# Taking the experts of a mixture-of-experts layer in an order computed on the chip

## The chip, the cores and the metric

The kernel runs on one core of one Trainium2 chip. The metric is device microseconds of one execution, from launch to end. One further execution was taken by the hardware profiler; its times count from the first instruction, and "span" is the time from the first to the last instruction. In the profile PE is the matrix engine (PEld its weight loads), DVE, ACT and POOL are the vector, scalar and general engines, and SP is the engine whose queue issues nearly all DMA loads here.

## The reference

One layer: a token mixer (gated delta rule and state-space heads), then a mixture of 32 experts, then a final RMSNorm. The mixer is not touched by the change. What matters is the expert layer, over 256 tokens of width 1024:

```
logits = (hf @ router_w + router_b).astype(jnp.float32)
top_logit, top_idx = lax.top_k(logits, TOP_K)          # TOP_K = 4 of N_EXPERTS = 32
gates = jax.nn.softmax(top_logit, axis=-1)
...
def expert_block(args):
    xb, e = args
    y = clamped_swiglu(xb @ w_gu[e] + b_gu[e])         # 1024 -> 2 x 1024, float32
    return y @ w_down[e] + b_down[e]                   # 1024 -> 1024
...
y_rows = y_rows * row_gate[:, None].astype(y_rows.dtype)
out = jax.ops.segment_sum(y_rows, row_tok, num_segments=n_tok + 1)[:n_tok]
```

256 tokens with 4 experts each make 1024 assignments, 32 to an expert on average; how many an expert gets is known only when the router has run. The sum over experts does not depend on the order in which they are taken.

## The kernel before

**Weights.** Each expert has 12 MiB of float32 weights, read once: eight loads of 1 MiB for gate and up (`w<-in_moe_w_gu_dram` in the profile), then four of 1 MiB for down (`w<-in_moe_w_down_dram`). `seq` lists all 384 loads, expert 0 to expert 31. `fetch(n)` issues them in that order on SP's queue (line L87 in the profile), each into the next of 20 slots of 1 MiB in turn (`SLOTS`). A load has to wait until the weights that stood in its slot have been used by PE. With 12 loads to an expert, 20 slots hold one whole expert and the first eight loads of the next. The last load is issued in two halves. The source address of each load is a constant of the program.

**The main loop.** It takes the experts one after the other, `e` from 0 to 31. `Block.pick` and `gather` select up to `CAP` = 64 tokens of an expert by a one-hot matrix made from `pos` (the token's place within the expert, 0 if it isn't there); `features` turns them into `xe`; `gate_up` runs k = 0 to 7 over the eight loads of gate and up (tiles `pG`, `pU`), and with the last use of each its slot is free; `swiglu` and `hidden` make `hTe`; `down` goes over the other four loads (tile `pY`), `result` and `scatter` add the result to the sum `acc`. The work on the next expert's tokens and the last one's result stands between `gate_up` and `down`, so that PE has something to do while `swiglu` runs. After the last expert there is the final norm and the store.

**Extra blocks.** An expert with more than 64 tokens needs a second pass. `xblk` holds, for each expert, the number of extra blocks of `XCAP` = 32 tokens, computed at the router from the counts; engines load it into registers, four experts at a time (`extra_blocks`). At the start of iteration `e` a conditional branch (L1465) runs `extra(e)` if that number is positive: gather, gate and up, swiglu, down, result and scatter of up to 32 more tokens, one step after the other, with the same weights of expert `e`. It stands ahead of the main `gate_up` of `e`, so all 12 slots of the expert stay taken until the main pass has used them. In the profile its down product goes to tile `pw` instead of `pY`. (`rest`, at the end, is for experts with more than 96 tokens.)

**Names.** `id3[:, e]` picks the expert's row of the biases, `gt[:, t, e]` holds the weights of the tokens for the expert.

Of the kernel before, what the change touches and what calls it, by code (L numbers as in the profile page):

```python
# [22 lines left out]
FT = mybir.dt.float32  # L23
I32 = mybir.dt.int32
BF = mybir.dt.bfloat16
FR = mybir.dt.float32r
AF = mybir.ActivationFunctionType
OP = mybir.AluOpType
PSUM = bass.MemoryType.PSUM
AX = mybir.AxisListType  # L30
# [6 lines left out]
NE = 32  # L37
EPS = 1e-6
CAP = 64
XCAP = 32  # L40
XMAX = (SEQ - CAP) // XCAP
RING = 8

SLOTS = ("w5", "w6", "w7", "w0", "w1", "g", "odd", "c", "hT", "s2", "s1", "even", "xd", "s3", "w2", "w3", "w4", "yh",
         "yl", "xT")
# [3 lines left out]
def trunk_kernel(ctx: ExitStack, tc: tile.TileContext, x, c, ada_w, ada_b, norm1_g, norm2_g, w_in,  # L49
# [3 lines left out]
    nc = tc.nc  # L53
    V, S, T, G = nc.vector, nc.scalar, nc.tensor, nc.gpsimd
# [18 lines left out]
    last_load = [None]  # L73
# [16 lines left out]
    gu_src = moe_w_gu.rearrange("o e (k p) n -> p (o e) k n", p=128)  # L90
    dn_src = moe_w_down.rearrange("o e (p k) n -> p (o e) k n", p=128)
    seq = [(e, i) for e in range(n_static) for i in range(12)]
    W = {}

    def fetch(n):

        while len(W) < min(n, len(seq)):
            e, i = seq[len(W)]
            src = gu_src[:, e, i] if i < 8 else dn_src[:, e, 2 * i - 16:2 * i - 14]
            W[e, i] = load(src, [2 * D] if i < 8 else [2, D], SLOTS[len(W) % len(SLOTS)], True,  # L100
                           2 if len(W) == len(seq) - 1 else 1)

# [9 lines left out]
    def ts(t):  # L112
        return slice(t * 128, t * 128 + 128)
# [47 lines left out]
    def tmp(n, dt=FT):  # L161
        taken[0] += n
        v = scratch[:, taken[0] - n:taken[0]]
        return v if dt is FT else v.bitcast(dt)
# [63 lines left out]
    V.tensor_tensor(x64, l64, s64, op=OP.bitwise_xor)  # L228
    l64f = const.tile([128, 64], FT)
    V.tensor_copy(l64f, l64)  # L230
    s64f = tmp(64)
    V.tensor_copy(s64f, s64)
    x64f = tmp(64)
# [41 lines left out]
    p = pg()  # L275
# [857 lines left out]
    dump("A2", A2)  # L1133


    id3 = const.tile([96, NE], BF)
    for j in range(3):
        V.tensor_copy(id3[32 * j:32 * j + 32], ident[0:NE, 0:NE])
# [82 lines left out]
    T.matmul(p[:, 0:32], before, sel[:, 0], start=True, stop=True)  # L1221
    T.matmul(p[:, 32:64], before, sel[:, 1], start=True, stop=False)
    posm = T.matmul(p[:, 32:64], ones, sel[:, 0], start=False, stop=True)


    nmax = fc.tile([1, 1], FT)
# [1 line left out]
    nblk = fc.tile([1, NE + 1], I32)  # L1228
    V.tensor_scalar(nblk[:, :NE], p[0:1, 64:96], float(CAP), float(XCAP - 1 - CAP), op0=OP.max, op1=OP.add)
    V.tensor_scalar(nblk[:, NE:], nmax, float(CAP), float(XCAP - 1 - CAP), op0=OP.max, op1=OP.add)  # L1230
    xblk = const.tile([1, NE + 2], I32)
    V.tensor_scalar(xblk[:, :NE + 1], nblk, XCAP.bit_length() - 1, None, op0=OP.arith_shift_right)
    V.tensor_scalar(xblk[:, NE + 1:], xblk[:, NE:NE + 1], 1.0, None, op0=OP.subtract)
    V.tensor_tensor(xblk[:, NE + 1:], xblk[:, NE + 1:], xblk[:, NE - 1:NE], op=OP.max)
    pos = rt("pos", pool=const)
    V.scalar_tensor_tensor(pos, p[:, :64].rearrange("p (t e) -> p t e", t=2), 1.0, sel, op0=OP.add, op1=OP.mult)
    V.tensor_tensor(gt, gt, sel, op=OP.mult)
# [16 lines left out]
    def pw(tag="pw"):  # L1254
        return pm.tile([128, 512], FT, name=tag, tag=tag)
# [135 lines left out]
    def extra_blocks(e):  # L1391


        n = min(e + GROUP, NE)
        return nc.values_load_multi_w_load_instructions(xblk[0:1, e:n + 2 * (n == NE)], min_val=0, max_val=XMAX)

    fetch(len(SLOTS))

# [2 lines left out]
            T.matmul(pacc[t][:, n], ident, xt[:, t, n * 512:n * 512 + 512], start=True, stop=True)  # L1401

    def block(e):
        return Block(lambda i: W[e, i], id3[:, e:e + 1])

    def extra_block(weights, pick, pcol, gcol):
        blk = Block(weights, pick, XCAP)
        blk.pick(pcol, gcol)
        blk.gather()
        blk.features()  # L1410
        blk.gate_up()
        blk.swiglu()
        blk.hidden()
        blk.down()
        blk.result()
        blk.scatter()

    def extra(e):
        pc = mk.tile([128, 2, 1], FT, name="pc")
        V.tensor_scalar(pc, pos[:, :, e:e + 1], float(CAP), None, op0=OP.subtract)  # L1420
        extra_block(lambda i: W[e, i], id3[:, e:e + 1], lambda t: pc[:, t], lambda t: gt[:, t, e:e + 1])

    def rest():

# [33 lines left out]
    for e in range(n_static):  # L1458
        fetch(12 * e + len(SLOTS))
        nxt = block(e + 1) if e + 1 < n_static else None  # L1460
        if nxt:
            nxt.pick(lambda t: pos[:, t, e + 1:e + 2], lambda t: gt[:, t, e + 1:e + 2])
        if e % GROUP == 0:
            nxs = extra_blocks(e)[1]
        with tc.If(nxs[e % GROUP if nxt else -1] > 0, label=f"more{e}", preferred_fallthrough_block=True):  # L1465
            if nxt:
                extra(e)
            else:
                with tc.If(nxs[e % GROUP] > 0):
                    extra(e)  # L1470
                with tc.If(nxs[-2] > 1):
                    rest()
        if not nxt:

            fgb = slot(SLOTS[4], "fgb")[:, :D]
            nc.sync.dma_start(fgb, final_g.rearrange("(o d) -> o d", o=1).to_broadcast([128, D]))
        if prev:
            prev.result()
        cur.gate_up()
        cur.swiglu()  # L1480

        if nxt:
            with tc.issue_after(cur.last.ins):
                tc.mark_branch_hint_location(f"more{e + 1}", engines=[nc.tensor.engine])
        if prev:
            with tc.issue_after(cur.last.ins):
                prev.scatter()
        if nxt:
            with tc.issue_after(cur.last.ins):
                nxt.gather()  # L1490
        cur.hidden()
        if nxt:
            nxt.features()
        cur.down()
        prev = cur
        cur = nxt
    if prev:
# [44 lines left out]
```

## Time and profile before

| | us |
|---|---|
| median of 3 runs | 1362.15 |
| the 3 runs | 1360.41, 1362.15, 1365.9 |
| the profiled execution | 1360.52 |
| its span | 1358.4 |
| start of the first expert's gate and up on PE, from the start of the span | 417.97 |
| end of the last matmul of the last expert's down | 1345.50 |
| PE busy | 1279.3 (94% of the span) |
| DVE, ACT busy | 541.0, 173.9 |
| moved by DMA | 470.21 MB, 346 GB/s over the span |

The first 418 us are the mixer and the router, the next 927 us are the 32 experts, and the last 13 us the final norm and the store. A busy PE in this profile can be a PE whose matmuls follow each other without a visible gap, whatever sets their pace, so the shares of busy time alone do not say what bounds the expert stage.

### The profile page before, as it was taken

The page shows a single profiled execution, that of the slowest core. Times are in us where ns is not written, and L with a number is a line of the kernel's source. Part 1 is how long each engine was busy: PE and PEld are TensorE (multiplying, and loading weights), DVE is VectorE, ACT ScalarE, POOL GpSimd, SP SyncE. Part 2 cuts the span into 40 slices and gives each one's busy share as a digit, 9 for nine tenths or more (in the row PEclk, how much of TensorE's full clock was granted, in tenths as well). Part 3 has the DMA queues.
Part 4 walks back from the last instruction along what each step waited for, and adds up shares of the span by engine and source line. Part 5 has one row for each costly group of instructions (what it writes and reads, how often), then busy time and mean ns, then how long its engine had stood idle before and what let it go on. Part 6 is the DMA issues. An engine that isn't in the chain of part 4 may idle for free. (4 is left out here: it accounts for less than half of the span.)

```text
span 1358.4 us, 18855 instructions
## 1 busy us (share of the span) xinstructions
PE 1279.3 (94%) x7520; PEld 625.9 (46%) x7521; DVE 541.0 (40%) x1555; ACT 173.9 (13%) x369; POOL 33.4 (2%) x46
## 2 busy tenths in 40 slices
PE   5999999999999999999998999998988999999996
PEld 3887787876553333333333333333333333333332
DVE  5797987444743223323322222222223223222322
ACT  1122222211210001000100001000000000000101
POOL 3010100000100000000000000000000000000000
PEclk9999999999998999999999999999999899999998
DMA  9986482316277999999999999999999999999991
GB/s 340 329 268 208 145 275 88 124 63 248 93 286 289 426 426 427 424 426 427 426 424 426 427 425 426 426 426 426 425 426 426 427 425 426 383 425 426 426 422 68
DMA packets 114450, 470.21 MB, mean 346 GB/s; under 512 B 7893, under 2 KB 59329, under 8 KB 65297
## 3 DMA queue, kind: packets, MB, share of 16 engines
q1 hardware_dynamic: 113120, 466.42, 84.7%
q10 hardware_dynamic: 704, 1.64, 0.4%
q8 instruction: 91, 1.49, 0.4%
q0 software_dynamic: 496, 0.35, 0.1%
q14 instruction: 39, 0.31, 0.1%
HBM read 466.74 MB, written 1.05 MB: 344 GB/s over the span
## 5 line engine op out<-in xcount | busy, mean ns | idle before, releaser
L1334 PE MATMUL pG<-w,xe 128*64 128x512 f32 (+1 forms) x1152 | 285.7, 584 | 15.1 <-DMA w<-in_moe_w_gu_dram 14.9
L1334 PE MATMUL pU<-w,xe 128*64 128x512 f32 (+1 forms) x1152 | 282.8, 578 | 0.0
L1362 PE MATMUL pY<-w,hTe 128*64 128x512 f32 x1024 | 225.2, 592 | 0.9 <-ACT hTe L1351 0.7
L338 PE MATMUL mm<-hT,w 128*128 128x256 f32 x800 | 200.1, 389 | 0.0
L1338 DVE TENSOR_SCALAR ga<-pG 128x512 f32<-128x512 f32 (+1 forms) x34 | 23.0, 676 | 411.1 <-PE pG L1334 411.1
L1334 PEld LDWEIGHTS pG<-w,xe 128*64 128x64 f32 (+1 forms) x1152 | 85.3, 136 | 156.4 <-issue 111.0
L1334 PEld LDWEIGHTS pU<-w,xe 128*64 128x64 f32 (+1 forms) x1152 | 88.1, 136 | 144.9 <-issue 141.7
L338 PEld LDWEIGHTS mm<-hT,w 128*128 128x128 f32 x800 | 142.6, 190 | 21.1 <-issue 2.9
L1362 PEld LDWEIGHTS pY<-w,hTe 128*64 128x64 f32 x1024 | 72.0, 137 | 132.7 <-issue 127.1
L1373 DVE SCALAR_TENSOR_TENSOR ye<-pY,gs,g2p 128x512 f32<-128x512 f32 (+1 forms) x33 | 24.1, 734 | 171.1 <-PEq L1465 162.1
L1340 ACT ACTIVATE th<-ga 128x512 f32<-128x512 f32 (+1 forms) x34 | 21.1, 620 | 470.4 <-DVE ga L1338 470.4
L1301 DVE TENSOR_SCALAR xe<-pw,A,sh 128x64 f32<-128x64 f32 (+1 forms) x272 | 70.9, 332 | 0.7 <-PE pw L1297 0.7
L1288 PE MATMUL pw<-xt,P 128*64 128x512 f32 (+1 forms) x288 | 64.0, 579 | 0.0
L1374 ACT ACTIVATE yh<-ye 128x512 fp32r<-128x512 f32 (+1 forms) x35 | 21.1, 606 | 278.4 <-DVE ye L1373 275.1
L367 DVE SCALAR_TENSOR_TENSOR t_c<-w,cact,t_c 128x256 f32<-128x256 f32 x112 | 52.2, 477 | 0.7
L1331 PE MATMUL pG<-bias,id 96*64 96x512 bf16 (+1 forms) x72 | 14.6, 413 | 24.8 <-PEq L1465 22.5
L506 DVE SCALAR_TENSOR_TENSOR t_c<-mm,cwg,t_c 128x255 f32<-128x255 f32 (+2 forms) x72 | 34.3, 477 | 7.8 <-ACT t_c L504 7.5
L1308 DVE TENSOR_SCALAR QT<-pU 128x256 fp32r<-128x256 f32 x32 | 13.6, 424 | 59.5 <-PE pU L1304 59.4
L1386 PE MATMUL acc<-yh,QT 64*128 64x512 f32 (+1 forms) x148 | 33.1, 422 | 3.2 <-ACT yh L1374 3.2
L1291 ACT ACTIVATE xg<-pw 128x512 f32<-128x512 f32 (+1 forms) x34 | 19.9, 585 | 104.6 <-PE pw L1288 104.6
L1349 PEld LDWEIGHTS pG<-ident,ga 128*128 128x128 f32 x132 | 18.5, 209 | 29.2 <-issue 29.0
L1288 PEld LDWEIGHTS pw<-xt,P 128*64 128x64 f32 (+1 forms) x288 | 16.8, 134 | 30.3 <-issue 29.5
(419 smaller groups left out, 1125.4 us busy)
## 6 DMA issues: line engine op xcount, KB each, us to landing
w<-in_moe_w_gu_dram SPq DMA_DIRECT2D x256, 1024.0 KB, 19.6
w<-in_moe_w_down_dram SPq DMA_DIRECT2D x127, 1024.0 KB, 19.5
w<-in_w_in_dram SPq DMA_DIRECT2D x26, 1024.0 KB, 5.9
w<-in_ada_w_dram SPq DMA_DIRECT2D x24, 1024.0 KB, 8.3
w<-in_w_out_dram SPq DMA_DIRECT2D x8, 1024.0 KB, 4.9
xt<-in_x_dram ACTq DMA_DIRECT2D x1, 1024.0 KB, 5.4
w<-in_moe_w_down_dram SPq DMA_DIRECT2D x2, 512.0 KB, 19.9
out_dram<-o SPq DMA_DIRECT2D x4, 256.0 KB, 2.0
```

Of the source, the lines that this page charges most:

```text
L338: T.matmul(job.p, self.w[:, k, ts(job.i)], hT[:, k], start=(k == 0), stop=(k == KT - 1))
L367: V.scalar_tensor_tensor(a, self.w[:, k], cact[:, k:k + 1], a, op0=OP.mult, op1=OP.add)
L506: V.scalar_tensor_tensor(acc[:, s:], p[:, :SEQ - s], wc(3 - s), acc[:, s:], op0=OP.mult, op1=OP.add)
L1288: T.matmul(p[self.rows(h), :self.wid], self.P[:, t], xt[:, t, self.cols(h)], start=(t == 0), stop=(t == 1))
L1301: V.tensor_scalar(xe[:, k], p[:, c0:c0 + cap], A2[:, k:k + 1], sh2[:, k:k + 1], op0=OP.mult, op1=OP.add)
L1334: self.last = T.matmul(dst, self.xe[:, k], hid(self.w(k), o, j), start=False, stop=(k == KT - 1))
L1338: V.tensor_scalar(ga, self.pG, 7.0, None, op0=OP.min)
L1340: S.activation(th, ga, AF.Tanh, scale=0.851)
L1362: T.matmul(pY[self.rows(n)], self.hT[:, k % self.nt, self.rows(k // self.nt)], self.w(8 + k // 2)[:, k % 2, self.cols(n)], start=False, st ...
L1373: V.scalar_tensor_tensor(ye[:, c], self.pY[:, c], self.gs, g2p[self.cap][:, c], op0=OP.mult, op1=OP.mult)
L1374: S.activation(self.yh[:, c], ye[:, c], AF.Copy)
L1386: T.matmul(dst, self.QT[n % 2][half_, t], part[half_, i * w:(i + 1) * w], start=False, stop=part is self.yl, skip_group_check=True)
```

## The change

The first four places (`FIRST`) keep experts 0 to 3. The other 28 places are filled by an order computed on the chip: of experts 4 to 31, those with more than 64 tokens are put from place 12 on, counting from 0 (`BUSY`; so from the thirteenth), and the others keep their order around them. The order is computed at the end of iteration 0 (`order_places`), and the tables of the main loop are permuted by it with a one-hot matrix `hot` in iteration 1: `posP`, `gtP`, `id3P` and `xblkP` stand for `pos`, `gt`, `id3` and `xblk` from place 4 on. `turns` holds the expert of each place. SP loads it into registers, four places at a time, and the weight loads from place 4 on take their source address from such a register.

```
+FIRST = 4
+BUSY = 12
...
     def fetch(n):
 
         while len(W) < min(n, len(seq)):
             e, i = seq[len(W)]
-            src = gu_src[:, e, i] if i < 8 else dn_src[:, e, 2 * i - 16:2 * i - 14]
+            if e < FIRST:
+                src = gu_src[:, e, i] if i < 8 else dn_src[:, e, 2 * i - 16:2 * i - 14]
+            else:
+                if e not in which:
+                    with tc.issue_after(last_load[0].ins):
+                        _, vs = nc.values_load_multi_w_load_instructions(
+                            turns[0][0:1, e:e + 4], engines=[nc.sync.engine], min_val=0, max_val=NE - 1)
+                    which.update({e + j: v for j, v in enumerate(vs)})
+                ds = bass.ds(which[e], 1)
+                src = (gu_src[:, ds, i].rearrange("p o n -> p (o n)") if i < 8 else
+                       dn_src[:, ds, 2 * i - 16:2 * i - 14].rearrange("p o k n -> p (o k) n"))
...
+    ecol = const.tile([32, 1], FT, name="ecol")
+    V.tensor_copy(ecol, pcol_i[0:32, 0:1])
...
+    S.activation(cnts, p[0:32, 64:96], AF.Copy)
...
-    xblk = const.tile([1, NE + 2], I32)
-    V.tensor_scalar(xblk[:, :NE + 1], nblk, XCAP.bit_length() - 1, None, op0=OP.arith_shift_right)
-    V.tensor_scalar(xblk[:, NE + 1:], xblk[:, NE:NE + 1], 1.0, None, op0=OP.subtract)
-    V.tensor_tensor(xblk[:, NE + 1:], xblk[:, NE + 1:], xblk[:, NE - 1:NE], op=OP.max)
+    xblk = const.tile([1, NE + 1], I32)
+    V.tensor_scalar(xblk, nblk, XCAP.bit_length() - 1, None, op0=OP.arith_shift_right)
...
+    def place(e):
+        return (pos if e < FIRST else posP)[:, :, e:e + 1]
...
+    def order_places():
+
+        x = mk.tile([32, 3, NE], FT, name="more", bufs=1)
+        r = mk.tile([32, 8], FT, name="places", bufs=1)
+
+        V.tensor_scalar(x[:, 0], cnts, float(CAP), None, op0=OP.is_gt)
+        V.memset(x[:, 0, 0:FIRST], 0.0)
+        V.tensor_reduce(r[:, 0:1], x[:, 0], op=OP.add, axis=AX.X)
+
+        for i in range(2):
+            V.tensor_tensor(x[:, 1 + i], x[:, 0], eye32[:, i], op=OP.mult)
+        V.tensor_reduce(r[:, 1:3], x[:, 1:3], op=OP.add, axis=AX.X)
...
+        V.tensor_tensor(r[:, 3:4], ecol, r[:, 2:3], op=OP.subtract)
+        V.scalar_tensor_tensor(r[:, 4:5], r[:, 3:4], float(BUSY), r[:, 0:1], op0=OP.is_ge, op1=OP.mult)
+        V.tensor_tensor(r[:, 3:4], r[:, 3:4], r[:, 4:5], op=OP.add)
+
+        V.tensor_scalar(r[:, 5:6], r[:, 0:1], -1.0, float(NE), op0=OP.mult, op1=OP.add)
+        V.scalar_tensor_tensor(r[:, 5:6], r[:, 5:6], float(BUSY), r[:, 2:3], op0=OP.min, op1=OP.add)
+        V.tensor_tensor(r[:, 5:6], r[:, 5:6], r[:, 3:4], op=OP.subtract)
+        V.scalar_tensor_tensor(r[:, 3:4], r[:, 5:6], r[:, 1:2], r[:, 3:4], op0=OP.mult, op1=OP.add)
+        hot = mk.tile([32, NE], FT, name="hot", bufs=1)
+        V.tensor_scalar(hot, l64f[0:32, 0:NE], r[:, 3:4], None, op0=OP.is_equal)
+        for j in range(3):
+            V.tensor_copy(id3P[32 * j:32 * j + 32], hot)
+        small.update(hot=hot, r=r)
+
+    def order_turn():
+
+        p = pw()
+        for i, v in enumerate((pos, gt)):
+            for t in range(2):
+                T.transpose(p[0:32, (2 * i + t) * 128:(2 * i + t + 1) * 128], v[:, t], ident)
+        pgT = small["pgT"] = mk.tile([128, 512], FT, name="th", bufs=1)[0:32]
+        S.activation(pgT, p[0:32], AF.Copy)
+
+    def order_apply():
+
+        hot, pgT, r = small["hot"], small["pgT"], small["r"]
+        p = pw()
+        for i in range(4):
+            T.matmul(p[:, i * 32:i * 32 + 32], pgT[:, ts(i)], hot, start=True, stop=True)
+        T.matmul(p[0:1, 128:160], ecol, hot, start=True, stop=True)
+        T.matmul(p[0:1, 160:192], r[:, 7:8], hot, start=True, stop=True)
+        S.activation(posP, p[:, 0:64].rearrange("p (t e) -> p t e", t=2), AF.Copy)
+        S.activation(gtP, p[:, 64:128].rearrange("p (t e) -> p t e", t=2), AF.Copy)
+        turn_ = mk.tile([1, NE], I32, name="turns", bufs=1)
+        V.tensor_scalar(turn_, p[0:1, 128:160], 0.0, None, op0=OP.add)
+        turns.append(turn_)
...
         if nxt:
             nxt.features()
+        if e == 1:
+            order_turn()
         cur.down()
+        if e < 2:
+            (order_places, order_apply)[e]()
```

Where the new instructions stand in the engines' programs is shown at three places. The first is PE in iteration 1, the second expert's `down`; before, it is one run of 16 products, followed by the branch of the next iteration:

```order
L1362 MATMUL pY<-w,hTe 64x512 x16
L1465 COMPARE_AND_BRANCH
```

After the change the four transposes of `pos` and `gt` stand inside that run, and the six products with `hot` behind it, ahead of the branch:

```order
L1381 MATMUL pY<-w,hTe 64x512 x7
L1473 MATMUL pw<-ident,pos 32x128 x2
L1473 MATMUL pw<-ident,gt 32x128 x2
L1381 MATMUL pY<-w,hTe 64x512 x9
L1482 MATMUL pw<-hot,th 128x32 x4
L1483 MATMUL pw<-hot,ecol 1x32
L1484 MATMUL pw<-hot,places 1x32
L1557 COMPARE_AND_BRANCH
```

The second is SP's queue around the first load of place 4, the 49th load; before, it is one of a run, and an expert's loads need nothing between them:

```order
L87 DMA w<-in_moe_w_gu_dram 128x2048 x7
L87 DMA w<-in_moe_w_down_dram 128x2048 x4
L87 DMA w<-in_moe_w_gu_dram 128x2048
L1465 COMPARE_AND_BRANCH
```

After it, the registers of four places are loaded ahead of it (ISA rows are register operations), and each load from there on has a register operation of its own; this repeats to the end:

```order
L90 DMA w<-in_moe_w_gu_dram 128x2048 x7
L90 DMA w<-in_moe_w_down_dram 128x2048 x4
L107 TENSOR_LOAD turns
L107 ISA x8
L90 ISA
L90 DMA w<-in_moe_w_gu_dram 128x2048
L1557 COMPARE_AND_BRANCH
L1557 UNCONDITIONAL_BRANCH x2
L90 ISA
L90 DMA w<-in_moe_w_gu_dram 128x2048
```

The third is DVE between the router and the first expert, from the first expert's `PG` to its `xe`; before:

```order
L1282 TENSOR_SCALAR PG<-slots_2815,pos,gt 128x128 x2
L1308 TENSOR_SCALAR QT<-pU 128x256
L1316 TENSOR_REDUCE gs_3380<-pU 128x1
L1301 TENSOR_SCALAR xe_3366<-pw,A_190,sh_191 128x64 x8
```

After the change the first steps of `order_places` stand there:

```order
L1301 TENSOR_SCALAR PG<-slots_2821,pos,gt 128x128 x2
L1444 TENSOR_SCALAR more<-cnts 32x32
L1494 COPY xblkP<-xblk 1x1
L1445 MEMSET more 32x4
L1495 TENSOR_SCALAR xblkP<-xblkP 1x1
L1446 TENSOR_REDUCE places<-more 32x1
L1449 TENSOR_TENSOR more<-more,eye_2814 32x32 x2
L1458 TENSOR_SCALAR places<-places 32x1
L1450 TENSOR_REDUCE places<-more 32x2
L1451 TENSOR_TENSOR more<-cnts,eye_2814 32x32
L1327 TENSOR_SCALAR QT<-pU 128x256
```

The other steps follow behind `xe` and between the next expert's `P` and `PG`. Nothing else changes its place by more than a few instructions.

## Rows read from the trace of the kernel before

**Rows 1.** Page, part 2: GB/s moved in 40 equal slices of the span

```profile
GB/s 340 329 268 208 145 275 88 124 63 248 93 286 289 426 426 427 424 426 427 426 424 426 427 425 426 426 426 426 425 426 426 427 425 426 383 425 426 426 422 68
```

**Rows 2.** PE by line, 417 to 1035 us, then 1064 to 1142.7: count | busy, mean | idle

```profile
L1362 PE MATMUL pY<-w,hTe 128*64 128x512 f32 x704 | 154.8, 592 | 0.2 <-ACTq L1465 0.2
...
L1362 PE MATMUL pY<-w,hTe 128*64 128x512 f32 x96 | 21.1, 592 | 0.0
```

**Rows 3.** PE timeline, the down products of seven experts: start, us, instructions

```profile
463.49 7.04 PE L1362 MATMUL pY<-w,hTe 128*64 128x512 f32 x32
...
489.80 7.04 PE L1362 MATMUL pY<-w,hTe 128*64 128x512 f32 x32
...
729.20 7.03 PE L1362 MATMUL pY<-w,hTe 128*64 128x512 f32 x32
...
1028.45 7.04 PE L1362 MATMUL pY<-w,hTe 128*64 128x512 f32 x32
...
1083.20 7.04 PE L1362 MATMUL pY<-w,hTe 128*64 128x512 f32 x32
...
1135.83 7.04 PE L1362 MATMUL pY<-w,hTe 128*64 128x512 f32 x32
...
1338.41 7.09 PE L1362 MATMUL pY<-w,hTe 128*64 128x512 f32 x32 [0.69 <-ACT hTe L1351]
```

**Rows 4.** Waits of PE, 700 to 1035 us: total us, times, longest

```profile
PE pG L1334 <- DMA w<-in_moe_w_gu_dram: 9.9, 21, 0.6
```

**Rows 5.** PE timeline, first main product after each extra block; extra's gate by line

```profile
1064.24 0.41 PE L1331 MATMUL pG<-bias,id 96*64 96x512 bf16 x2
...
1162.41 0.41 PE L1331 MATMUL pG<-bias,id 96*64 96x512 bf16 x2
...
L1334 PE MATMUL pG<-w,xe 128*32 128x256 f32 (+1 forms) x66 | 5.9, 404 | 5.0 <-DMA w<-in_moe_w_gu_dram 5.0
```

**Rows 6.** SP timeline: start of the first and length to the last of x loads

```profile
1033.55 7.70 SPq L87 DMA_DIRECT2D w<-in_moe_w_down_dram  x4
...
1145.36 5.23 SPq L87 DMA_DIRECT2D w<-in_moe_w_gu_dram  x3
...
1164.81 5.48 SPq L87 DMA_DIRECT2D w<-in_moe_w_down_dram  x4
...
1291.50 7.70 SPq L87 DMA_DIRECT2D w<-in_moe_w_gu_dram  x4
```

**Rows 7.** Issue to landing, us, of loads issued at 420.5, 1001.7 (1150.3 alike), 1040.9, 1168.2, 1298.8

```profile
w<-in_moe_w_down_dram SPq DMA_DIRECT2D x1, 1024.0 KB, 4.7
...
w<-in_moe_w_gu_dram SPq DMA_DIRECT2D x1, 1024.0 KB, 19.6
...
w<-in_moe_w_down_dram SPq DMA_DIRECT2D x1, 1024.0 KB, 19.6
...
w<-in_moe_w_down_dram SPq DMA_DIRECT2D x1, 1024.0 KB, 8.9
...
w<-in_moe_w_gu_dram SPq DMA_DIRECT2D x1, 1024.0 KB, 19.7
```

**Rows 8.** PE timeline, last up products of expert 21 and of the last expert

```profile
1022.82 1.05 PE L1334 MATMUL pU<-w,xe 128*64 128x512 f32 x4
...
1333.75 1.05 PE L1334 MATMUL pU<-w,xe 128*64 128x512 f32 x4
```

**Rows 9.** SP's instructions by line, ns min/median/max: register loads, register operations, load issues

```profile
L1395 SPq FUSED_REGOPS  x34: 147/147/178, 409.3 to 1243.7; - x34
L1395 SPq TENSOR_LOAD <-xblk x8: 295/302/738, 408.7 to 1241.4; - x8
...
L87 SPq DMA_DIRECT2D w<-in_moe_w_gu_dram x256: 327/328/653, 267.3 to 1298.9; - x128
```

**Rows 10.** DVE timeline at the router and the first expert, with idle time and its end

```profile
404.92 0.16 DVE L1211 TENSOR_TENSOR eq<-eq,ngt 128x2 f32<-128x2 f32 x1
...
414.15 0.42 DVE L1308 TENSOR_SCALAR QT<-pU 128x256 fp32r<-128x256 f32 x1 [3.06 <-PE pU L1304]
```

More of the change, by code (lines that the diff above doesn't have):

```diff
@@ L92, in trunk_kernel @@
     seq = [(e, i) for e in range(n_static) for i in range(12)]
-    W = {}
+    W, which, turns = {}, {}, []
     def fetch(n):
@@ L1133, in trunk_kernel @@
     dump("A2", A2)
+    cnts = const.tile([32, NE], FT, name="cnts")
+    eye32 = const.tile([32, 2, NE], FT, name="eye32")
+    V.tensor_copy(eye32[:, 0], ident[0:32, 0:32])
+    V.tensor_copy(eye32[:, 1], after[0:32, 0:32])
     id3 = const.tile([96, NE], BF)
@@ L1394, in extra_blocks @@
         n = min(e + GROUP, NE)
-        return nc.values_load_multi_w_load_instructions(xblk[0:1, e:n + 2 * (n == NE)], min_val=0, max_val=XMAX)
+        return nc.values_load_multi_w_load_instructions((xblk if e < FIRST else small["xblk"])[0:1, e:n + 2 * (n == NE)], min_val=0, max_val=XMAX)
     fetch(len(SLOTS))
@@ L1403, in block, with ident_of, share @@
     def block(e):
-        return Block(lambda i: W[e, i], id3[:, e:e + 1])
+        return Block(lambda i: W[e, i], ident_of(e))
+    def ident_of(e):
+        return (id3 if e < FIRST else id3P)[:, e:e + 1]
+    def place(e):
+        return (pos if e < FIRST else posP)[:, :, e:e + 1]
+    def share(e, t):
+        return (gt if e < FIRST else gtP)[:, t, e:e + 1]
+    small = {}
+    posP = mk.tile([128, 2, NE], FT, name="posP", bufs=1)
+    gtP = mk.tile([128, 2, NE], FT, name="gtP", bufs=1)
@@ new lines, in trunk_kernel @@
+    id3P = mk.tile([96, NE], BF, name="id3P", bufs=1)
+    def order_places():
[7 more added lines that the diff above has]
+        V.tensor_reduce(r[:, 1:3], x[:, 1:3], op=OP.add, axis=AX.X)
+        V.tensor_tensor(x[:, 0], cnts, eye32[:, 0], op=OP.mult)
+        V.tensor_reduce(r[:, 7:8], x[:, 0], op=OP.add, axis=AX.X)
+        V.tensor_tensor(r[:, 3:4], ecol, r[:, 2:3], op=OP.subtract)
[10 more added lines that the diff above has]
+        small.update(hot=hot, r=r)
@@ new lines, in order_turn @@
+    def order_turn():
[17 more added lines that the diff above has]
+        turns.append(turn_)
+        nb = mk.tile([1, NE], I32, name="nb", bufs=1)
+        V.tensor_scalar(nb, p[0:1, 160:192], float(CAP), float(XCAP - 1 - CAP), op0=OP.max, op1=OP.add)
+        xb = small["xblk"] = mk.tile([1, NE + 2], I32, name="xblkP", bufs=1)
+        V.tensor_scalar(xb[:, :NE], nb, XCAP.bit_length() - 1, None, op0=OP.arith_shift_right)
+        V.tensor_copy(xb[:, NE:NE + 1], xblk[:, NE:NE + 1])
+        V.tensor_scalar(xb[:, NE + 1:], xb[:, NE:NE + 1], 1.0, None, op0=OP.subtract)
+        V.tensor_tensor(xb[:, NE + 1:], xb[:, NE + 1:], xb[:, NE - 1:NE], op=OP.max)
@@ L1419, in extra @@
         pc = mk.tile([128, 2, 1], FT, name="pc")
-        V.tensor_scalar(pc, pos[:, :, e:e + 1], float(CAP), None, op0=OP.subtract)
-        extra_block(lambda i: W[e, i], id3[:, e:e + 1], lambda t: pc[:, t], lambda t: gt[:, t, e:e + 1])
+        V.tensor_scalar(pc, place(e), float(CAP), None, op0=OP.subtract)
+        extra_block(lambda i: W[e, i], ident_of(e), lambda t: pc[:, t], lambda t: share(e, t))
     def rest():
@@ L1461, in trunk_kernel @@
         if nxt:
-            nxt.pick(lambda t: pos[:, t, e + 1:e + 2], lambda t: gt[:, t, e + 1:e + 2])
+            nxt.pick(lambda t: place(e + 1)[:, t], lambda t: share(e + 1, t))
         if e % GROUP == 0:
```

## The prediction

> **What bounds the kernel now.** I read the slices of the page first. From slice 14 on the loads run at 426 GB/s without a break [rows 1]; the one slice with 383 is looked at below. An expert's 12 loads are 12.58 MB, so the stream of weights takes 29.5 us an expert, 2.46 us a load. Next, PE's pace: down products start 26.31 us apart while nothing holds PE up (463.49 to 489.80), but from 729.20 to 1028.45, ten experts, the mean step is 29.9 [rows 3], and there PE waits for weights 21 times [rows 4]. So PE alone is faster than the stream by 3.2 us an expert. It begins behind a full ring of slots, catches up by the twelfth expert (place 11, counting from 0), and then follows the stream.
>
> Then the extra blocks. The first stretch of [rows 2] has 704 down products of 32 to an expert: 22 experts, places 0 to 21, before the first extra block; the second has 96, places 22 to 24. Extra blocks thus stand at places 22 and 25, so experts 22 and 25 are the only ones over 64 tokens, and the new order puts them at places 12 and 13, with the rest in their old order.
>
> What did they cost? I measure how far the end of an expert's down lies behind the landing of its last load. SP's row at 1033.55 ends with the twelfth load of place 22, issued at 1033.55 + 7.70 - 0.33 = 1040.92, landing 19.6 later, at 1060.5 [rows 6, 7]; place 21's was 29.5 earlier, 1031.0. PE ended place 21 at 1028.45 + 7.04 = 1035.49, 4.5 behind, and place 22 at 1090.24, **29.7 behind** [rows 3]. Part of that first extra was waiting for weights (5.0 us in its gate product alone, [rows 5]), since it began with PE up to date. The second took from 1135.83 + 7.04 = 1142.87 to 1162.41, 19.5 us, with none of this [rows 3, 5].
>
> Did the stream stop? Until main place 25 releases its first slot, no load of place 26's down can go out: after 1145.36 + 5.23 SP issues nothing until 1164.81 [rows 6]. That is the slice of 383. But a load counts as landed when its slowest part has landed: the last one before the hole was issued at 1150.26 and landed at 1169.9, and the third after it, issued at 1164.81 + 2 x 1.72 = 1168.25, at 1177.1 [rows 6, 7]. Three loads in 7.2 us is the stream's own pace. The slowest part of the queue never ran dry, and the stream ended when it would have ended without extras. Only PE was late.
>
> How late? Place 31's eighth load was issued at 1291.50 + 7.70 - 0.33 = 1298.87 and landed at 1318.6 [rows 6, 7]. At place 21, in step with the stream, that load landed at 1001.7 + 19.6 = 1021.3 and the down ended 14.2 later. The last expert has less between up and down: 1338.41 - 1333.75 = 4.66 against 1028.45 - 1022.82 = 5.63 [rows 3, 8]. So in step its down would end at 1318.6 + 14.2 - 1.0 = 1331.8. It ended at 1345.50. **13.7 us** is what the two late extras cost.
>
> **The change part by part.**
>
> *Moving the extras* to places 12 and 13 leaves 18 experts behind them at 3.2 us each, 58 us, to catch up. PE will be 29.7 + 19.2 - 3.2 = 45.7 behind after place 13 and needs some 12 experts, so it is in step by about place 25. The 13.7 come back.
>
> *A new stall of the stream.* Before, two experts stood between the extras, and PE had won back 6.4 us when the second came. Now none stand between. Count from the landing of place 12's last load. PE ends place 12 at +29.7; the second extra and the first step of place 13's gate and up release a slot 1164.81 - 1142.87 = 21.9 later, at +51.6. The 20 slots hold 20 more loads, landed at +49.2. The 21st should land at +51.7, but is issued only at +51.6, and a load that finds an empty queue takes 4.7 [rows 7]: +56.3. The stream stops for **4.6 us**, and since it bounds the end again, all of it counts. The Trainium skill (DMA: Bandwidth & Descriptors, section Anatomy of one DMA) has 2.0 us plus bytes over 436 GB/s for one DMA, 4.4 for this one; that would make the stall 4.3. It was fitted on another queue than SP's, and the row decides.
>
> *Register addresses.* 337 loads get a register operation, 0.147 each, beside 0.33 for the issue [rows 9]; seven times SP loads four registers, 0.3 plus four checks, about 1 us. SP has 2.46 us a load and up to eight loads (19.6 us) queued ahead, so nothing shows. How long an issue from a register takes, no row tells: nothing more at the low end, 0.65 (the longest of these issues) at the high one, and at that too the cost is 0. It would matter from 2.3 us on.
>
> *Computing the order.* DVE gets some 25 instructions of 0.16 [rows 10]. Eleven stand ahead of the first expert's `QT`, about 2 us in a hole of 3.06, in which PE gathers the first expert's tokens: 0, and up to 2 if PE got there sooner. The copy of the counts on ACT now stands ahead of DVE's block counts, a few tenths; two small DVE instructions went there: 0, within 0.5 either way, and that would count in full. On PE, ten small operations in iteration 1: from nothing up to 20 instructions of 0.59 (mean of the far larger down products, [rows 2]), 11.8 us; being smaller, I take 3. PE's reserve covers it: the step into place 11 has 2.6 us of waiting in it, and the first extra 5.0, so up to about 7 costs nothing, and the far end some 4.
>
> *The first registers.* SP reads `turns` ahead of the 49th load, which goes out around 480 with several loads queued; `turns` comes after place 1's down at 463.49 + 7.04 = 470.5, plus about 3 for the added work and a few tenths for the copy: 474. No wait.
>
> **Sum.** -13.7 + 4.6 = -9.1 us, on the profiled execution's 1360.52 (span 1358.4): 1351.4. The median of the runs lies 1.6 above that execution; from 1362.15 I get **1353.0**.
>
> **Rivals.**
> 1. *No stall.* If the second extra begins with PE less than 25 behind, the refill comes in time and all 13.7 are won: 1348.5. Against it: the first extra ends tied to its last load's landing, whatever the place. 0.08.
> 2. *A longer stall.* Each microsecond that the extras, the refill or the work in iteration 1 take more than I assumed counts in full. 5 us more (the far end for PE's added work, say) gives 1358. 0.15.
> 3. *Nothing gained:* PE isn't in step by the end. It would take about 19 us more delay (six experts in hand at 3.2), which nothing here shows; or the stall eats the gain, 9 us more. 1360 to 1364. 0.06.
> 4. *Slower: the stream loses pace with register addresses.* 337 loads; if each takes 0.03 us more, the gain is gone, and at 0.1 more the kernel needs 34 - 9 = 25 us more, 1387. For it: no load in this trace takes its address from a register, so the pace is not shown. Against it: SP waits most of the 2.46 us, and the descriptors that the DMA engines get are of the same shape. 0.09.
>
> My forecast has 0.62. About 0.5% is what a measurement of this kernel tells from no change, 6.8 us: faster means under 1355.3. Forecast and rival 1 are faster, with a little of rival 2: 0.72. Most of rival 2 and rival 3 are within: 0.19. Slower: 0.09. The range goes from rival 1, 1348, to the middle of rival 2's tail, 1359; left out are rival 4 and the ends of 2 and 3. The likeliest case alone spans 1351 to 1355.5.
>
> **What would show it.** Extra blocks at places 12 and 13 (around 740 and 790 us from the start of the span). PE steps of 26.3 from there to about place 25, then 29.5 with waits for weights. One pause of 4 to 5 us in the landings around 815, and 426 GB/s otherwise. The last load landing some 5 us later than before, the last down ending about 9 earlier, around 1336.4. I am wrong if the slices after 418 us are under 425 GB/s (rival 4), if the pause is missing or over 8 us, or if PE is still more than 5 us behind at the last expert.

## The result, and the profile after

The changed kernel is slower: 1373.64 us (median of 4 runs, 1371.04 to 1374.57) against 1363.36 for the kernel before, ratio 1.0064 [1.0048, 1.0081]. The forecast was 1353.0, with 1348 to 1359 as its range, so the time lies outside it and on the other side. The profiled execution took 1371.04 us (span 1369.3), where the prediction had 1351.4.

I read the profile in the order of the prediction's own list of signs. First where the extra blocks stand. PE's timeline, down products of main places in `pY`, of extra blocks in `pw` (start, us, instructions):

```profile
738.17 7.04 PE L1381 MATMUL pY<-w,hTe 128*64 128x512 f32 x32
...
772.95 1.07 PE L1381 MATMUL pw<-w,hTe 128*32 128x256 f32 x16 [1.10 <-DMA w<-in_moe_w_down_dram]
...
795.64 7.04 PE L1381 MATMUL pY<-w,hTe 128*64 128x512 f32 x32
...
815.87 3.66 PE L1381 MATMUL pw<-w,hTe 128*32 128x256 f32 x64 [0.53 <-ACT hTe L1370]
...
841.14 7.04 PE L1381 MATMUL pY<-w,hTe 128*64 128x512 f32 x32
...
1077.95 7.04 PE L1381 MATMUL pY<-w,hTe 128*64 128x512 f32 x32
...
1348.79 7.09 PE L1381 MATMUL pY<-w,hTe 128*64 128x512 f32 x32 [0.69 <-ACT hTe L1370]
```

These are the downs of place 11, the first extra, place 12, the second extra, places 13, 22 and 31. From 841.14 to 1077.95 are nine places of 26.31 us, PE's own pace; from there to 1348.79 nine of 30.1, the stream's. So the extras moved as the order says, PE worked off its delay and was in step again from place 22 or 23 on, where the forecast had about 25; with a slower stream it has less to catch up. The mechanism is the forecast one. But the last down ended at 1348.79 + 7.09 = 1355.88, not at 1336.4.

Next the pause of the stream. SP's timeline around it and at the end, then issue to landing of the load issued at 1322.5:

```profile
785.96 17.22 SPq L90 DMA_DIRECT2D w<-in_moe_w_gu_dram  x8
824.59 5.48 SPq L90 DMA_DIRECT2D w<-in_moe_w_down_dram  x4
...
1319.99 2.82 SPq L90 DMA_DIRECT2D w<-in_moe_w_gu_dram  x2
```

```profile
w<-in_moe_w_gu_dram SPq DMA_DIRECT2D x1, 1024.0 KB, 19.7
```

The eighth load of place 14 was issued at 785.96 + 17.22 - 0.33 = 802.85 and, with an issue to landing of 19.7 like the one shown, landed at 822.5. The next could go out only at 824.59, when place 13's gate and up had released a slot, and the third after the pause landed at 835.4 (read from the trace, which lacks the landings of the first two): 12.8 us for three loads that take 7.4 at the pace around them, a pause of 5.4 (forecast: 4.6).

The eighth load of the last expert landed at 1319.99 + 2.82 - 0.33 + 19.7 = 1342.2. Before it was 1318.6 [rows 6, 7]. So the stream ends 23.6 us later, where the forecast had 4.6, and the slices of the page say why:

```profile
GB/s 312 287 290 202 173 261 111 93 94 230 108 238 312 420 420 420 420 420 420 420 420 420 421 382 361 420 420 420 420 420 420 419 421 420 420 420 420 420 421 197
```

419 to 421 GB/s in every undisturbed slice, against 424 to 427 [rows 1]. Over the 888 us that the stream took before (from about 430, when the first loads landed that had waited for a slot, to 1318.6), 426/420 costs 12.7 us. With 5.4 for the pause and 4.3 for a later begin (place 1's down starts at 467.82 instead of 463.49 [rows 3]) this makes 22.4 of the 23.6; the other 1.2 are not accounted for. PE's timeline, the downs of places 1 and 2 (that of place 1 has the four transposes inside it):

```profile
467.82 3.60 PE L1381 MATMUL pY<-w,hTe 128*64 128x512 f32 x14
471.90 4.51 PE L1381 MATMUL pY<-w,hTe 128*64 128x512 f32 x18
...
497.89 7.04 PE L1381 MATMUL pY<-w,hTe 128*64 128x512 f32 x32
```

A slower stream was rival 4's sign, so register addresses look guilty. Two views speak against it. SP's instructions at the loads and at `turns` (ns, min/median/max):

```profile
L90 SPq FUSED_REGOPS  x337: 42/46/56, 488.2 to 1332.8; - x169
L90 SPq DMA_DIRECT2D w<-in_moe_w_gu_dram x256: 327/333/680, 274.4 to 1322.5; - x128
L90 SPq MOVE w<-in_moe_w_gu_dram x224: 29/29/29, 488.4 to 1322.4; - x112
...
L107 SPq TENSOR_LOAD <-turns x7: 296/298/308, 486.8 to 1212.0; - x7
```

Register work is cheap (0.046 + 0.029 us a load), the issue 5 ns longer than before [rows 9]. And the first registers are loaded at 486.8, with some 20 us of loads queued; what the DMA engines moved from 440 to 500 us had almost entirely been issued earlier than that, from constant addresses. Before, then after:

```profile
DMA packets 3501, 25.52 MB, mean 425 GB/s; under 512 B 391, under 2 KB 391, under 8 KB 391
DMA packets 3460, 25.22 MB, mean 420 GB/s; under 512 B 386, under 2 KB 386, under 8 KB 386
```

The stream is slow already there. My theory after this: the change adds three tiles to the pool `const`, which lies ahead of the ring in SBUF: `ecol` (4 bytes a partition, rounded to 32), `cnts` (128) and `eye32` (256), 416 in all. In the built programs the 20 slots begin at byte 36608 of each partition before, and at 37024 after, 8192 apart in both. 36608 is a multiple of 256; 37024 is one of 32 only. Theory A: the place of the slots sets the pace. Theory B: the register addresses, or another part of the changed program. Theory C: the chip on which the comparison ran.

### The profile page after: what moved, and what is told of

Its sections match the earlier page's. It is cut to its first block, busy times and chain, and to the rows that moved or that the text cites. A ratio compares the mean times of both kernels' runs of the same rounds, so it can differ in the third digit from the quotient of the medians.

```text
span 1369.3 us, 19655 instructions
## 1 busy us (share of the span) xinstructions
PE 1282.8 (94%) x7536; PEld 631.1 (46%) x7537; DVE 544.0 (40%) x1581; ACT 175.1 (13%) x373; POOL 33.4 (2%) x46
## 5 line engine op out<-in xcount | busy, mean ns | idle before, releaser
L1350 PE MATMUL pG<-bias,id3P 96*64 96x512 bf16 (+1 forms) x64 | 12.8, 411 | 21.2 <-PEq L1557 21.2
## 6 DMA issues: line engine op xcount, KB each, us to landing
w<-in_moe_w_gu_dram SPq DMA_DIRECT2D x256, 1024.0 KB, 19.7
w<-in_moe_w_down_dram SPq DMA_DIRECT2D x127, 1024.0 KB, 19.7
```

## The experiments

In the diffs, lines that stay are left out. Every time is a median, every ratio is to the kernel before on the same chip.

**The kernel before, with slots moved.** One tile is added ahead of the ring and nothing uses it; its size is the only difference between four kernels (8, 16, 32 and 64 columns are 32, 64, 128 and 256 bytes a partition):

```
     V.tensor_copy(l64f, l64)
+    pad = const.tile([32, 8], FT, name="pad")
+    V.memset(pad, 0.0)
```

> The kernel before, with one unused tile of 32 bytes a partition among the constants, so that the 20 ring slots (and the pools behind them) begin 32 bytes further on: at 36640 instead of 36608, an odd multiple of 32, as after the change (37024). Experts in their own order, constant addresses. Theory A (the place of the slots sets the stream's pace): a load every 2.48 us instead of 2.452, so 364 x 0.03 = 11 us more, and some 4 us more ahead of the first expert: 1373 to 1379 us. Theory B (loads with an address from a register, or another part of the changed program, slow the stream): 1360 to 1366 us, as before, 2.45 us a load. Theory C (the chip of the first comparison): 1360 to 1366 us here, and the changed kernel no slower on this chip.

> The control of the shift by 32 bytes: the same unused tile with 64 bytes a partition, the slots at 36672, again a multiple of 64. Theory A, if it is the multiple of 64 that counts: 1360 to 1366 us and 2.45 us a load. Theory A, if any move of the slots or the former multiple of 256 counts: 1373 to 1379 us, as with 32 bytes. Theories B and C: 1360 to 1366 us.

> The kernel before with an unused tile of 128 bytes a partition among the constants: ring slots from 36736, a multiple of 128 but not of 256 (before: 36608, a multiple of 256; 36640 and 36672 took 2.49 us a load instead of 2.452, and 1378 and 1376 us). If a multiple of 128 is enough: 2.45 us a load, 1360 to 1366 us. If it takes a multiple of 256, or if 36608 itself or the one more instruction matters: 2.48 to 2.49 us a load, 1374 to 1380 us.

> The same with 256 bytes: ring slots from 36864, a multiple of 256 (and of 512, as 36608 is not). If a multiple of 128 or of 256 is what counts: 2.45 us a load, 1360 to 1366 us. If the stream is slow here too, the alignment is not the cause, but the moved pools, the one more instruction or the place 36608 itself: 2.48 to 2.49 us a load, 1374 to 1380 us.

| slots begin at | multiple of | time, us | ratio | loads 48 to 99, us each |
|---|---|---|---|---|
| 36608 (before) | 256 | 1363.4 to 1364.6 | 1 | 2.452 |
| 36640 (+32) | 32 | 1378.07 | 1.0108 [1.0076, 1.0139] | 2.494 |
| 36672 (+64) | 64 | 1376.10 | 1.0100 [1.0083, 1.0116] | 2.484 |
| 36736 (+128) | 128 | 1375.51 | 1.0093 [1.0064, 1.0122] | 2.483 |
| 36864 (+256) | 256 | 1365.45 | 1.0015 [0.9998, 1.0033] | 2.440 |

The last column is the median spacing of landings in the one profiled execution, loads counted from 0 (where the trace lacks a landing, the space to the next one is shared out). The page's slices for +32, +64, +128 and +256, in this order:

```profile
GB/s 313 286 294 200 166 270 100 92 93 244 93 263 315 419 418 419 416 419 420 417 420 417 420 418 418 420 417 419 417 418 421 417 419 418 371 419 418 419 416 102
```

```profile
GB/s 308 288 287 202 176 257 114 92 93 234 103 245 293 419 421 420 420 419 420 420 421 419 421 420 420 421 420 420 421 419 421 420 420 419 385 420 420 420 417 109
```

```profile
GB/s 307 322 278 216 140 278 94 111 75 246 92 286 298 421 421 420 420 420 421 419 421 420 422 419 421 420 420 421 420 420 422 420 420 420 369 420 421 420 418 90
```

```profile
GB/s 340 289 284 209 150 280 94 95 92 246 94 252 314 426 425 426 425 426 426 425 425 425 426 426 426 425 426 426 426 426 426 426 425 426 383 425 426 425 414 55
```

This shows A, without B or C: the kernel before, in its own order, with constant addresses, loses 11.5 to 13.5 us when its slots move by 32, 64 or 128 bytes, and next to nothing when they move by 256. My first guess, a multiple of 64, was wrong; of the steps tried only 256 is enough. How far off the multiple the slots are makes little difference (2.483 to 2.494). The transfers of 500 to 700 us show where the time is, first for +128, then for +256 (queue: packets, MB, share of 16 engines):

```profile
q1 hardware_dynamic: 11500, 83.74, 100.8%
```

```profile
q1 hardware_dynamic: 11653, 84.86, 100.7%
```

In both the 16 DMA engines are busy all the time; with +128 they get 1.3% fewer packets done, so each packet takes longer.

**The same tile behind the ring.** Slots at 36608 again, all pools behind them moved by 32:

```
+    late = ctx.enter_context(tc.tile_pool(name="late", bufs=1))
...
+    pad = late.tile([32, 8], FT, name="pad")
+    V.memset(pad, 0.0)
```

> The kernel before with the unused tile of 32 bytes a partition behind the ring instead of ahead of it: the slots stay at 36608, every tile of the pools behind the ring moves on by 32 bytes. If the slots alone count: 2.45 us a load, 1361 to 1367 us, and some 340 GB/s in the first slice. If other tiles' places count too: a slower stream (2.48 us a load), or a first expert that starts some 3 us later, and 1367 to 1377 us.

1363.94 us, ratio 0.9989 [0.9968, 1.0009], 2.452 us a load; the slices:

```profile
GB/s 348 268 293 200 161 275 98 93 94 242 98 248 289 425 427 425 425 425 426 425 426 425 426 425 426 426 426 425 425 426 426 427 426 425 380 425 426 425 417 60
```

So it is not the tiles behind the ring, nor the one instruction more. The constants laid out after the added tile move together with the slots in all four kernels above; the packets that take longer are those of the loads into the slots, and the kernel with 37120 below separates part of the rest. The first slice follows the slots too: 339 to 348 GB/s with slots at a multiple of 256, 306 to 313 otherwise, in all fourteen profiles; the mixer's weights are loaded into the same ring.

**The changed kernel with slots moved.** `ecol`'s tile is made wider, to 64 bytes (16 columns, slots at 37056, a multiple of 64) or to 128 (32 columns, 37120, a multiple of 256); or the three new tiles go to a pool behind the ring (36608):

```
-    ecol = const.tile([32, 1], FT, name="ecol")
+    ecol = const.tile([32, 32], FT, name="ecol")[:, 0:1]
```

```
+    late = ctx.enter_context(tc.tile_pool(name="late", bufs=1))
...
-    ecol = const.tile([32, 1], FT, name="ecol")
+    ecol = late.tile([32, 1], FT, name="ecol")
...
-    cnts = const.tile([32, NE], FT, name="cnts")
-    eye32 = const.tile([32, 2, NE], FT, name="eye32")
+    cnts = late.tile([32, NE], FT, name="cnts")
+    eye32 = late.tile([32, 2, NE], FT, name="eye32")
```

> The changed kernel, with ecol's tile 64 bytes a partition instead of 4 (rounded to 32), so that the slots begin at 37056, a multiple of 64. Everything else as changed: computed order, 337 register addresses, extra blocks at places 12 and 13. Theory A: 2.45 us a load, 11.3 us less of stream and up to 4.3 us less ahead of the first expert, so 1357 to 1363 us; the 5.5 us pause of the stream at place 14 stays. Theory B: 1371 to 1375 us, with loads of 2.48 us. Theory C: the same as the changed kernel has on this chip.

> The changed kernel with ecol's tile 128 bytes a partition, so that the slots begin at 37120, a multiple of 256 again (512 on from 36608). Order, register addresses and extra blocks as changed. If the alignment of the slots is the whole of the slower stream: 2.45 us a load for constant and for register addresses alike, 11 to 13 us less than with 37056 (1370.4 us), so 1357 to 1361 us. If register addresses or something else of the changed program slow the stream too: the loads from place 4 on stay over 2.46 us, and the time over 1364 us.

> The changed kernel with its three new tiles for constants (ecol, cnts, eye32) in a pool of their own behind the ring, so that the slots begin at 36608 as before, and all that lies behind them is moved. Order, register addresses and extra blocks as changed (places 12 and 13). If the slots alone count: 2.45 us a load and the time of the changed kernel with slots at 37120, 1353 to 1357 us. If the tiles behind count too: 1360 to 1370 us.

| slots begin at | time, us | ratio | loads 48 to 99, us each |
|---|---|---|---|
| 37056 | 1370.36 | 1.0055 [1.0034, 1.0076] | 2.486 |
| 37120 | 1354.99 | 0.9948 [0.9927, 0.9969] | 2.450 |
| 36608 (tiles behind) | 1356.18 | 0.9927 [0.9897, 0.9957] | 2.437 |

With 37056, expected by A as I then had it to be good, the stream stayed slow, in line with the control above. With either way of putting the slots at a multiple of 256 the changed kernel is faster than the one before, by what the order wins. 1354.99 lies a little under the 1357 to 1361 expected, so the step from 37056 is worth more than the 11 to 13 I gave it (the two ran on different chips). The constants between `ecol` and `cnts` lie 128 bytes further on with 37120, if tiles are laid out in the order of the program; they do so in the kernel before with +128 too, and there the stream is slow. So their place isn't the cause. The ones behind `eye32` move only together with the slots in every run; that they play no part is not shown, though no weight load writes to them. The page's slices for 37056, then for 37120, and from the timelines of 37120 the pause on SP and the last down:

```profile
GB/s 306 327 278 212 146 280 94 98 88 246 93 261 312 420 419 419 420 419 421 420 418 420 421 380 369 420 419 419 419 420 419 420 420 420 421 420 420 419 420 215
```

```profile
GB/s 340 287 289 204 156 278 97 94 94 238 103 240 279 426 425 427 425 426 424 427 425 426 426 398 327 426 425 426 425 426 425 425 426 427 426 426 426 425 425 205
```

```profile
782.35 17.10 SPq L90 DMA_DIRECT2D w<-in_moe_w_gu_dram  x8
821.01 5.48 SPq L90 DMA_DIRECT2D w<-in_moe_w_down_dram  x4
...
1338.58 7.09 PE L1381 MATMUL pY<-w,hTe 128*64 128x512 f32 x32 [0.69 <-ACT hTe L1370]
```

The pause is longer here: landings at 816.8 and, three loads on, 832.4 make 8.3 us over the pace; 7.1 with the tiles behind the ring. This execution (1360.8 us) is the longest of its seven.

**The extras late again.** Slots at 37120, all instructions of the change, only the place number as late as before:

```
-BUSY = 12
+BUSY = 22
```

> The changed kernel with slots at 37120 and the busy experts at the 23rd and 24th place (BUSY 22 instead of 12): the same program, the same added instructions, only the place of the extra blocks is as late as before the change. If the gain comes from taking them early, it is gone: 9 to 12 us more than with BUSY 12 (1355.0 us), so 1364 to 1368 us, the last expert's down products some 18 us behind the last load instead of 4 to 5. If the gain had come from somewhere else in the changed program: 1353 to 1357 us.

1362.54 us, ratio 0.9991 [0.9973, 1.0010]: 7.5 us more than with 12 (which ran on another chip), 6.4 more than with the tiles behind the ring (same chip), and no gain over the kernel before. So the gain is the place of the extras and nothing else in the program. It is under the 9 to 12 expected, and the last down lies 12.4 us behind the landing of (the first half of) the last load, not 18: with the two side by side the stream pauses here as well (the slice of 311), which ends the loads later without ending PE later.

```profile
GB/s 341 279 290 202 159 278 96 93 94 242 98 246 289 426 424 426 426 425 425 426 425 425 426 426 426 426 426 426 426 425 426 427 311 422 426 424 427 426 424 140
```

```profile
1343.27 7.09 PE L1381 MATMUL pY<-w,hTe 128*64 128x512 f32 x32 [0.69 <-ACT hTe L1370]
```

**The extras apart.** The second and later busy experts are taken three places further on, so that PE can win back some 9 us between the two. `r[:, 3:4]` is a quiet expert's number among the quiet ones, `r[:, 2:3]` a busy one's among the busy ones:

```
+APART = 3
...
-        V.scalar_tensor_tensor(r[:, 4:5], r[:, 3:4], float(BUSY), r[:, 0:1], op0=OP.is_ge, op1=OP.mult)
+        V.tensor_scalar(r[:, 6:7], r[:, 0:1], 1.0, None, op0=OP.min)
+        V.scalar_tensor_tensor(r[:, 4:5], r[:, 3:4], float(BUSY), r[:, 6:7], op0=OP.is_ge, op1=OP.mult)
+        V.tensor_tensor(r[:, 5:6], r[:, 0:1], r[:, 6:7], op=OP.subtract)
+        V.scalar_tensor_tensor(r[:, 5:6], r[:, 3:4], float(BUSY + APART), r[:, 5:6], op0=OP.is_ge, op1=OP.mult)
         V.tensor_tensor(r[:, 3:4], r[:, 3:4], r[:, 4:5], op=OP.add)
+        V.tensor_tensor(r[:, 3:4], r[:, 3:4], r[:, 5:6], op=OP.add)
...
-        V.tensor_scalar(r[:, 5:6], r[:, 0:1], -1.0, float(NE), op0=OP.mult, op1=OP.add)
-        V.scalar_tensor_tensor(r[:, 5:6], r[:, 5:6], float(BUSY), r[:, 2:3], op0=OP.min, op1=OP.add)
+        V.tensor_scalar(r[:, 5:6], r[:, 2:3], 1.0, float(APART), op0=OP.min, op1=OP.mult)
+        V.scalar_tensor_tensor(r[:, 5:6], r[:, 5:6], float(BUSY), r[:, 2:3], op0=OP.add, op1=OP.add)
```

> The changed kernel with the slots at 37056 again, and the second busy expert taken three places later (extra blocks at places 12 and 16 instead of 12 and 13; the first still at the 13th place). The PE makes up some 3 us a place, so it is about 40 us behind the stream after place 16 instead of 45, and the pause of the stream at place 14 is gone. Theory A: 4 to 6 us less than with the extra blocks side by side: 1352 to 1358 us. If the pause does not reach the end of the kernel: the same as side by side. Theory B: 1366 to 1371 us.

> The same slots at 37120 with the extra blocks at places 12 and 16: the changed order with neither the slower stream nor the pause at place 14. If both are as read: 1363.1 us (the same order with slots at 37056) less 11 to 13, so 1350 to 1353 us, faster than both kernels. If the stream stays slow: 1361 to 1365 us.

With slots at 37056: 1363.14 us, ratio 0.9999 [0.9982, 1.0016]; with 37120: 1348.52 us, ratio 0.9902 [0.9869, 0.9935], the shortest median of all runs here and a little under the 1350 to 1353 expected. At 37056 it missed its range (1352 to 1358) by the stream that had been taken for cured there, but it is 7.2 us under the same slots with the extras side by side; at 37120 it is 6.5 under. So the pause does reach the end of the kernel, and it goes away. The slices for 37120, and PE's timeline with the second extra (place 16) and the last down:

```profile
GB/s 339 334 262 221 136 283 96 97 92 244 101 235 318 426 424 426 425 425 426 426 426 425 426 426 425 425 410 426 425 426 426 425 425 426 426 426 425 426 425 202
```

```profile
882.11 5.35 PE L1382 MATMUL pw<-w,hTe 128*32 128x256 f32 x64 [0.54 <-ACT hTe L1371]
...
1322.33 7.09 PE L1382 MATMUL pY<-w,hTe 128*64 128x512 f32 x32 [0.69 <-ACT hTe L1371]
```

The two slices of 398 and 327 are gone; one of 410, behind the second extra, is left. After place 16 PE is 36.8 us behind (read from the trace), less than the ring's 49, and it is in step by the end: the last down ends 4.1 after the landing of (the first half of) the last load.

**Constant addresses.** The order is computed and used as before, but the loads take the experts that it names from a list in the program. SP loads no expert numbers into registers and works out no addresses. The rest is the kernel with the extras apart and slots at 37120:

```
+ORDER = [*range(12), 22, 12, 13, 14, 25, *range(15, 22), 23, 24, *range(26, 32)]
...
-                ds = bass.ds(which[e], 1)
-                src = (gu_src[:, ds, i].rearrange("p o n -> p (o n)") if i < 8 else
-                       dn_src[:, ds, 2 * i - 16:2 * i - 14].rearrange("p o k n -> p (o k) n"))
+                x = ORDER[e]
+                src = gu_src[:, x, i] if i < 8 else dn_src[:, x, 2 * i - 16:2 * i - 14]
```

> The changed kernel with slots at 37120 and extra blocks at places 12 and 16 (1348.5 us), its loads given the constant addresses of the experts that the computed order names: no values loaded into SP's registers, no addresses worked out there; the order is still computed and used for all else. If register addresses cost nothing, as the prediction took them: the same within 3 us, 1345.5 to 1351.5 us, and 2.45 us a load. If they cost 0.01 us a load or more: 3 us less or still faster.

1348.74 us, ratio 0.9879 [0.9845, 0.9913], where the same with registers took 1348.52. SP's rows at the loads hold no register operation, and the issue takes 328 instead of 333 ns:

```profile
L92 SPq DMA_DIRECT2D w<-in_moe_w_gu_dram x256: 327/328/787, 267.6 to 1299.4; - x128
```

An address from a register costs nothing that these runs can tell: the intervals of the two ratios, from two chips, overlap, and the slices read 424 to 426 GB/s with either, away from the extras. Rival 4 needed 0.03 us a load, 10 us, to eat the gain; that is out.

## Why the prediction was wrong

**The step that failed** is the pace in the sum: -13.7 + 4.6 keeps the stream at its old 2.46 us a load, because the change part by part asks for the cost of added instructions and of addresses alone. The three tiles added to `const` have no entry there. Their 416 bytes move every slot of the ring off a multiple of 256, and the loads then run 1.2 to 1.7% slower, whatever the address they are read from. The prediction took the stream at 426 GB/s throughout; in the profile the 420 cost 12.7 of the 19.5 us by which the last down came later than forecast. In the runs a move off the multiple costs 11.5 to 13.5 us in the kernel before, and 15.4 (37056 against 37120, on two chips) in the changed one. The Trainium skill has the rule that would have raised the question (DMA: Bandwidth & Descriptors, section How a descriptor splits into AXI transactions): a descriptor is cut into transactions of 256 bytes, and where it does not start at a multiple of 256, its first one starts at the multiple below, and the bytes ahead of the start are fetched unused and still cost beats. Here the threshold agrees. The size does not, and the measurement decides: by the page's count of 32-byte beats, a row of 8 KB (256 beats) would cost 1, 2 and 4 more at offsets of 32, 64 and 128, an estimate of 0.4, 0.8 and 1.6%, growing with the offset; measured were 1.7, 1.3 and 1.3%. The page tells it of reads; what moved here is the place that is written. So the runs show the dependence on the place, and why a write there takes longer stays open.

**Rival 4** had the right sign, slices under 425, and the wrong cause. The number of loads times a few hundredths of a microsecond was the right form of loss, and register addresses were the only thing in view that touched all loads.

**What bounds the kernel**, the delay of 13.7 us and the places of the extras held. *Moving the extras* won about what was forecast, but only together with a stream at its old pace: with slots at a multiple of 256 the changed kernel takes 1354.99 or 1356.18 us, forecast 1353.0.

**The new stall** was mis-sized. Its begin was right: the 21st load went out 51.7 us after place 12's last load had landed (772.9 to 824.6 in the changed kernel), forecast +51.6. Its end was not: I let the first load take the 4.7 us of an empty queue and the next two follow at the pace, 9.6 for three; the third landed 10.8 after the first was issued, and 11.4 (37120) and 11.7 (tiles behind the ring) in the two kernels with the faster stream. That makes 5.4, and there 8.3 (1.6 of it from a first extra that much longer than before) and 7.1. With the extras side by side at the 23rd and 24th place it was 10.8 again, at the faster pace, so the pace does not set it. The prediction's rows hold no price for this: after the hole of the kernel before the third load landed 12.3 after the first issue [rows 6, 7], but there a load from before the hole was still 5.1 from landing. Why a refill takes 1.1 to 2.1 longer than 4.7 and two loads at the pace no run here shows. The stall's 2.5 to 3.7 us over the forecast are about what the forecast misses in the kernels with the old pace.

**Costs put at 0.** *Register addresses*: confirmed, by SP's rows (75 ns of register work a load, where I took 147) and by constant addresses. *PE in iteration 1*: from place 1's down to place 2's it took 30.07 us instead of 26.31, so 3.8 where I took 3; at its last down before the first extra PE was 3.7 behind the landing, as in the kernel before (3.8, read from both traces), so the waits had covered it. At the old pace with 37120 it was 4.5. *The first registers*: SP read them at 486.8, between two loads issued 2.0 apart: no wait. *The order on DVE and the counts on ACT*: not settled. The first expert's gate and up began 4.3 us later than before, but in the variants of the changed program it began anywhere from 414.9 to 423.3, and in the kernel before with moved slots from 419.1 to 426.4. One profiled execution of each cannot tell a cost of under 5 us there from this spread. The changed kernel's own 1373.64 against 1370.36 at 37056, with the same pace, lies in it too.

## What to carry to other kernels

A change also moves what is allocated behind it: where a kernel is bound by its loads, compare the start addresses of the load buffers in the built programs before and after, and keep them at a multiple of 256 bytes a partition (shown here for loads of 8 KB rows), most simply by allocating them ahead of everything whose size may change. When a stream slows down in all stretches alike, look first for a stretch that the suspected edit does not touch; here the loads with constant addresses cleared the register addresses in the first profile. Work that makes an engine late is best put where the engine has time to catch up, and two such pieces far enough apart that the buffer bridges each.

## What the runs showed of the hardware

- Weight loads of 1 MiB (128 rows of 8 KB) into slots at a multiple of 256 bytes a partition move 424 to 427 GB/s in the slices that nothing disturbs; at 32, 64, 128, 160 or 192 bytes off it 416 to 422, with little dependence on how far. PE's step of 26.31 us, where nothing holds it up, is the same in both, so it is the transfer and not the use of the data. Why an offset of 32 (2.494 us a load) is a little worse than the others (2.483 to 2.486) no run here shows.
- Taking a load's address from a register cost the issue 5 ns (333 instead of 328) and 46 + 29 ns of register operations on SP, and the transfer nothing that shows (slices of 424 to 426 GB/s with either).
- A queue that ran empty needed 10.7 to 11.7 us from the first issue until its third load of 1 MiB had landed (five profiles), although a single one takes 4.7 [rows 7].
